# One core's decoder layer: order of the first loads, TensorE in program order, and the last norm's column product

## The chip, the cores and the metric

The kernel runs on one core of a Trainium2 chip. Five engines work from queues of their own: TensorE (PE: matmuls, with weight loads on PEld), VectorE (DVE), ScalarE (ACT), GpSimd (POOL) and SyncE (SP, which issues the loads and stores). The metric is the device time of one execution in microseconds; lower is better. Matmul operands come from on-chip memory (SBUF), sums are kept in eight banks of PSUM.

## The reference

One layer on x of 512 tokens by 1024, in float32:

```
x = x + 0.5 * SwiGLU_1(RMSNorm(x))
h = RMSNorm(x);  P = h @ W_in
A = NSA attention (compressed, selected and sliding-window branch, 16 heads)
B = W_conv_out(Bg * conv3(Cg * xin))
x = x + W_out(sigmoid(ga) * (A @ W_nsa_out) + sigmoid(gb) * B)
x = x + 0.5 * SwiGLU_2(RMSNorm(x))
out = RMSNorm(x)      # x * rsqrt(mean(x^2) + eps) * gain
```

A SwiGLU is silu(x @ w_gate) * (x @ w_up), then @ w_down, with 2816 features (22 blocks f0 to f21 of 128).

## The kernel before, in words

x is held transposed: eight tiles d0 to d7 of 128 features by 512 tokens. Each float32 operand is split into a high part, rounded on ACT (`whi`, `hi`, `gh`), and the rest, taken on DVE (`wlo`, `lo`, `gl`); a product is the sum hi*hi + hi*lo + lo*hi, three matmuls to one chunk of 128.

The first feed-forward takes f0 to f3 as plain products. For g0, u0 and g1 the function `first` loads weights and x piece by piece, in the order of a list `items`, splits each as it comes and issues a matmul as soon as its row of weights and x are there. From f4 on, and for all of the second feed-forward, gate and up of one block f are computed together by a scheme of Strassen's kind, called here a quartet: seven half-size block products, in the written order a11, s1, s2, s3, a12, s4, a22, of 12 matmuls of 256 columns each, on four PSUM banks p1, p5, p6, p7. DVE makes the weights' sums (`ws`) and their low parts, joins the products (u, y, e) and multiplies by the norm's scale. Two things set waits: s4 adds to bank p5, from which u (line 553) reads the product s1, so s4 must come behind u; and a quartet's weights sit in pools of two or three buffers.

A norm is: squares on ACT, added up by DVE into `ssum`; a column product on PE (`col`) that sums over the partitions; v on DVE; the power -1/2 on POOL; a split of the result into rh and rl on DVE; and PE matmuls that spread it over the partitions (`rbp`). The scale is put on a product's output, so a product need not wait for its norm.

The last product (`down`, d7) is done in two halves of 256 tokens, each followed by its part of the norm (`final`) and eight outputs, two to a store of 256 KB.

What sets the order: every engine takes its instructions in the order in which they were queued. In the first parts of the two feed-forwards (`begin1`, `begin2`) that is the order of the code, by `manual_schedule`; elsewhere a scheduler orders each engine's instructions by its own costs, and may put blocks of the next quartets ahead of a block that it thinks late. In `begin2`, whose quartet f0 holds the middle norm, hooks 3, 4 and 5 put the norm's steps between the blocks. SP's loads keep the list's order.

Of the kernel before, what the change touches and what calls it, by code (L numbers as in the profile page):

```python
# [13 lines left out]
ENGINES = {mybir.EngineType.PE, mybir.EngineType.DVE, mybir.EngineType.Activation}  # L14
# [28 lines left out]
def f32(ap):  # L43
    return ap.bitcast(F32)


class Kernel:
# [17 lines left out]
    def fixed(self):  # L65

        const = self.const
        self.small = const.tile([P, SM_N], F32, name="small")
        self.one = const.tile([P, 1], F32, name="one")
        self.ident = const.tile([P, P], F32, name="ident")  # L70
        self.mhalf = const.tile([P, 4], F32, name="mhalf")
        self.identr = const.tile([P, P], F32R, name="identr")
        const.tile([P, PAD], F32, name="pad")
# [18 lines left out]
    def gemm(self, ps, chunks, xs, stepwise=False):  # L92
# [17 lines left out]
    def chain(self, ps, ops):  # L110
        for n, (w, x) in enumerate(ops):
            self.nc.tensor.matmul(ps, w, x, start=n == 0, stop=n == len(ops) - 1)  # L112
# [20 lines left out]
    def constants(self):  # L133
        nc = self.nc
        nc.scalar.dma_start(out=self.small, in_=self.io["small"])
        nc.vector.memset(self.one, 1.0)
# [8 lines left out]
        nc.gpsimd.tensor_copy(self.identr, self.ident)  # L145
# [9 lines left out]
    def square(self, x, d, c=slice(0, S)):  # L155
        nc = self.nc
        if d == 0:
            self.ssum = self.slot(name="ssum")
            nc.scalar.activation(self.ssum, x, AF.Square)
        else:  # L160
            sq = self.slot(name="sq")
            nc.scalar.activation(sq[:, c], x[:, c], AF.Square)
            nc.vector.tensor_add(self.ssum[:, c], self.ssum[:, c], sq[:, c])

    def rnorm(self, blocks=range(4)):

        steps = self.rnorm_steps(blocks)
        r = next(steps)
        next(steps)
        return r, next(steps)  # L170

    def rnorm_steps(self, blocks=range(4)):
        nc = self.nc
        b0, b1 = blocks[0], blocks[-1] + 1
# [6 lines left out]
        yield r  # L181
        hi, lo = (self.tmp.tile([P, 4], F32R, name=n, bufs=2) for n in ("rh", "rl"))
        nc.vector.tensor_copy(hi[:, b0:b1], r[:, b0:b1])
        nc.vector.tensor_sub(lo[:, b0:b1], r[:, b0:b1], f32(hi[:, b0:b1]))
        yield

        def spread():
            rb = self.ps.tile([P, S], F32, tag="ps", name="rbp")
            for b in blocks:
                self.chain(rb[:, b * P:(b + 1) * P],  # L190
                           [(t[:, b:b + 1].to_broadcast([P, P]), self.identr) for t in (hi, lo)])
            return rb

        yield spread
# [12 lines left out]
    def ffn1(self):  # L207

        nc, wgu = self.nc, self.io["wgu1"]
        rb = self.slot(name="rb")  # L210
        with self.tc.tile_pool(name="st", bufs=2) as self.st:
            with self.tc.manual_schedule(engines=ENGINES):
                hid, now = self.begin1(wgu, rb)
            self.tiles(wgu, now, hid, PLAIN, rb)
        self.xg, self.xf = [], {}
        self.down(self.io["wd1"], hid, rb, 1)

    def begin1(self, wgu, rb):
# [3 lines left out]
        out["g0"], out["u0"], out["g1"] = self.first([wgu[0, :, 0], wgu[0, :, 1], wgu[1, :, 0]])  # L222
# [24 lines left out]
        spread = self.rnorm()[1]  # L247
        product("u1", self.pmm, "mm")
        rbp = spread()
# [32 lines left out]
    def ffn2(self):  # L282
# [5 lines left out]
        with self.tc.tile_pool(name="st", bufs=2) as self.st:  # L288
            merged, now = self.merge(wgu, parts)
            self.xg = []  # L290
            rb = self.slot(name="rb")
            with self.tc.manual_schedule(engines=ENGINES):
                now = self.begin2(wgu, merged, now, rb, hid)
            self.tiles(wgu, now, hid, 1, rb)
# [23 lines left out]
    def begin2(self, wgu, merged, now, rb, hid):  # L318
# [29 lines left out]
        norm = self.rnorm_steps()  # L348

        def end():  # L350
            nc.scalar.copy(rb, next(norm)())

        hid.append(self.quartet(now[0], later[1], True, rb, {3: lambda: next(norm), 4: lambda: next(norm), 5: end}))
# [11 lines left out]
    def down(self, wd, hid, rb, nxt):  # L365
        nc = self.nc
        hs = []
        for d in range(KD):
# [6 lines left out]
            last = d == KD - 1 and nxt is None  # L375
            for c in ((slice(0, 256), slice(256, S)) if last else (slice(0, S),)):
                ps = self.pmm.tile([P, S], F32, tag="mm", name="dn")
                self.gemm(ps[:, c], chunks, [(h[:, c], l[:, c]) for h, l in hs], d == 0)
                x, t = self.x[d], self.slot(name="dt")
                nc.vector.tensor_mul(t[:, c], ps[:, c], rb[:, c])  # L380
                nc.vector.scalar_tensor_tensor(x[:, c], t[:, c], 0.5, x[:, c], op0=ALU.mult, op1=ALU.add)
                if last:
                    self.square(x, d, c)
                    self.final(c)
            if not last:
                self.residual(d, nxt)
# [143 lines left out]
    def quartet(self, w, steps, odd, rb, hooks):  # L530
# [23 lines left out]
        more()  # L554
        self.block(p7, w["s3"], "t3", True)
        hook(3)
# [3 lines left out]
        hook(4)  # L560
# [4 lines left out]
        hook(5)  # L565
        if hooks:
            nc.vector.tensor_mul(g[:, c0], half(p1), rb[:, c0])
        add(e[:, c1], u[:, c0], half(p5))
        nc.vector.tensor_mul(g[:, c1], e[:, c1], rb[:, c1])
        nc.scalar.activation(g, g, AF.Silu)  # L570
        self.block(p7, w["a22"], "t4", False)
        add(y[:, c0], u[:, c0], half(p7))
# [3 lines left out]
    def first(self, srcs):  # L576
# [10 lines left out]
        def load_w(t, k, n):  # L587
            raws[t, k, n] = raw = self.slot(name="w0")[:, :n * P]
            nc.sync.dma_start(out=raw, in_=srcs[t][:, k * P:(k + n) * P])
# [7 lines left out]
        for kind, *args in items:  # L597
# [4 lines left out]
            else:  # L602
                t, k, n = args
                hi, lo = self.split(raws[t, k, n], n=n * P)
                for j in range(n):
                    ws[t, k + j] = hi[:, j * P:(j + 1) * P], lo[:, j * P:(j + 1) * P]
# [133 lines left out]
    def keys_compressed(self, hid):  # L740
# [13 lines left out]
        self.chain(ps[:, :64], ops)  # L754
# [37 lines left out]
    def quad(self, n):  # L792
# [12 lines left out]
        self.chain(st, [(k[:, g, 96 - 32 * h:224 - 32 * h], self.qs[4 * n + h]) for h in range(4) for k in self.kc])  # L805
# [145 lines left out]
    def mixing(self):  # L951
# [3 lines left out]
        self.r, spread = self.rnorm()  # L955
        kc = self.proj(0)
        self.rb = self.slot(name="rb")
        nc.scalar.copy(self.rb, spread())
# [90 lines left out]
    def final(self, c):  # L1049
        nc = self.nc  # L1050
        rb = self.rnorm(range(c.start // P, c.stop // P))[1]()
        for d in range(0, KD, 2):
            o = self.slot(name="o").rearrange("p (d t) -> p d t", d=2)
            for j in range(2):
                nc.vector.scalar_tensor_tensor(o[:, j], self.x[d + j][:, c], self.gain(3, d + j), rb[:, c],
                                               op0=ALU.mult, op1=ALU.mult)
            nc.sync.dma_start(out=self.io["out"][d:d + 2, :, c].rearrange("d p t -> p d t"), in_=o)
# [57 lines left out]
```

## Time and profile before

| | |
|---|---|
| median of 3 runs | 1299.24 us (1299.22 to 1299.62) |
| the profiled execution | 1299.69 us |
| its span, first to last instruction | 1297.9 us |
| mean granted clock of TensorE | 0.996 |
| PE busy | 1282.4 us, 99% |
| DVE, ACT, POOL busy | 965.8, 613.1, 9.3 us |
| the chain that ended last | PE 97%, DVE 1%, DMA 1% |

Busy time is the time in which an engine had work; the granted clock is TensorE's, as a share of 2.4 GHz. A timeline row has the start, the duration and, in brackets, the idle time before it and the instruction that ended it. Matmul durations overlap: the distance of two starts is the pace, not the duration.

### The profile page before, as it was taken

What the parts mean: (1) busy time and instruction counts of PE and PEld (TensorE: products, weight loads), DVE (VectorE), ACT (ScalarE), POOL (GpSimd) and SP (SyncE); (2) the same over time, 40 slices, a digit from 0 to 9 for tenths busy, and PEclk for the clock granted to TensorE, in tenths of its full rate; (3) what the DMA queues carried; (4) which work ended last, traced back from release to release, by engine and by line L of the source; (5) the groups of instructions that cost most, each with busy time, mean ns of one, the idle gap of its engine ahead of it and who ended that gap; (6) DMA issues with size and microseconds to landing.
All of it is one profiled execution on the core that took longest, in us unless ns stands there. A gap on an engine that the chain in (4) does not pass through costs nothing.

```text
span 1297.9 us, 19392 instructions
## 1 busy us (share of the span) xinstructions
PE 1282.4 (99%) x7660; PEld 1139.7 (88%) x7660; DVE 965.8 (74%) x1790; ACT 613.1 (47%) x1039; POOL 9.3 (1%) x33
## 2 busy tenths in 40 slices
PE   9999999999999999999999999999999999999996
PEld 7899999888888988888888888888899999998886
DVE  7899999834376377787787767766799999986334
ACT  7644444622245455555555547634544444454220
POOL 1000000000000000000000000000000000000000
PEclk9999999999999999999999999999999999999999
DMA  5233333343425422122121111243223333333321
GB/s 197 90 122 98 102 111 109 99 122 106 126 83 173 136 68 81 50 65 65 55 76 49 66 66 49 65 130 121 91 92 104 99 113 100 112 94 102 95 84 65
DMA packets 38987, 124.39 MB, mean 96 GB/s; under 512 B 4336, under 2 KB 6768, under 8 KB 38896
## 3 DMA queue, kind: packets, MB, share of 16 engines
q1 hardware_dynamic: 38752, 123.09, 29.8%
q8 instruction: 60, 0.98, 0.3%
q14 instruction: 31, 0.25, 0.1%
q10 hardware_dynamic: 144, 0.06, 0.0%
HBM read 118.94 MB, written 4.19 MB: 95 GB/s over the span
## 4 chain that ended last, share of the span: by engine, by line
PE 97%; DVE 1%; DMA 1%; ACT 0%; POOL 0%; SPq 0%; issue 0%; POOLq 0%; DVEq 0%
PE st L528 30%; PE pj L112 22%; PE dn L112 19%; PE yb L112 3%; PE wo L112 3%; PE ya L112 3%; PE s L857 3%; PE pt L882 3%; PE gu L112 2%; PE pv L900 2%; PE pv L899 2%; PE gu L612 1%; PE sct L112 1%; DMA w<-wgu 0%; PE nat L667 0%; PE nat L668 0%
## 5 line engine op out<-in xcount | busy, mean ns | idle before, releaser
L86 ACT CAST whi<-wraw 128x1024 fp32r<-128x1024 f32 (+2 forms) x140 | 143.0, 1022 | 243.5 <-PE dn L112 105.9
L87 DVE TENSOR_TENSOR wlo<-wraw,whi 128x1024 fp32r<-128x1024 f32 (+2 forms) x140 | 165.9, 1185 | 103.9 <-PE dn L112 67.9
L528 PE MATMUL st<-xf,whi 128*128 128x256 f32 x1248 | 228.4, 283 | 0.5 <-DVE u L553 0.5
L528 PEld LDWEIGHTS st<-xf,whi 128*128 128x128 f32 x1248 | 194.7, 192 | 0.7 <-DVE u L553 0.7
L528 PE MATMUL st<-xf,wlo 128*128 128x256 f32 x624 | 176.7, 283 | 0.0
L112 PE MATMUL pj<-hi,whi 128*128 128x512 f32 x416 | 165.1, 397 | 0.0
L112 PE MATMUL pj<-lo,whi 128*128 128x512 f32 x416 | 163.0, 392 | 0.0
L112 PE MATMUL dn<-hi,whi 128*128 128x512 f32 (+1 forms) x374 | 139.6, 378 | 0.0
L112 PE MATMUL dn<-lo,whi 128*128 128x512 f32 (+1 forms) x374 | 138.8, 377 | 0.0
L528 PE MATMUL st<-xf,gh 128*128 128x256 f32 x640 | 119.8, 284 | 1.0 <-ACT gh L431 1.0
L528 PEld LDWEIGHTS st<-xf,wlo 128*128 128x128 f32 x624 | 119.7, 192 | 0.5 <-DVE wlo L435 0.4
L431 ACT CAST whi<-ws 128x1024 fp32r<-128x1024 f32 x78 | 81.1, 1048 | 64.1 <-DVE ws L447 60.6
L112 PE MATMUL pj<-hi,wlo 128*128 128x512 f32 x416 | 102.9, 389 | 0.0
L528 PEld LDWEIGHTS st<-xf,gh 128*128 128x128 f32 x640 | 100.4, 192 | 1.6 <-ACT gh L431 1.4
L435 DVE TENSOR_TENSOR wlo<-ws,whi 128x1024 fp32r<-128x1024 f32 x78 | 95.0, 1217 | 0.3 <-ACT whi L431 0.2
L112 PE MATMUL dn<-hi,wlo 128*128 128x512 f32 (+1 forms) x374 | 94.9, 377 | 0.0
L112 PEld LDWEIGHTS pj<-hi,wlo 128*128 128x128 f32 x416 | 78.0, 188 | 16.2
L528 PE MATMUL st<-xf,gl 128*128 128x256 f32 x320 | 90.6, 284 | 0.8 <-DVE gl L435 0.8
L112 PEld LDWEIGHTS pj<-lo,whi 128*128 128x128 f32 x416 | 78.2, 188 | 14.5
L112 PEld LDWEIGHTS pj<-hi,whi 128*128 128x128 f32 x416 | 78.2, 188 | 14.5 <-ACT hi L129 0.4
L863 ACT ACTIVATE p<-p,st 128x512 f32<-128x512 f32 (+3 forms) x128 | 70.3, 552 | 28.0 <-DVE st L860 28.0
L112 PEld LDWEIGHTS dn<-lo,whi 128*128 128x128 f32 x374 | 70.4, 188 | 13.8 <-DVE lo L127 0.7
(249 smaller groups left out, 2451.8 us busy)
## 6 DMA issues: line engine op xcount, KB each, us to landing
wraw<-wgu SPq DMA_DIRECT2D x83, 512.0 KB, 3.6
wraw<-win SPq DMA_DIRECT2D x52, 512.0 KB, 3.5
wraw<-wd SPq DMA_DIRECT2D x32, 512.0 KB, 3.5
wraw<-wd SPq DMA_DIRECT2D x16, 384.0 KB, 3.2
wraw<-cw SPq DMA_DIRECT2D x8, 512.0 KB, 3.8
wraw<-wconv SPq DMA_DIRECT2D x8, 512.0 KB, 3.4
wraw<-wnsa SPq DMA_DIRECT2D x8, 512.0 KB, 3.6
wraw<-wout SPq DMA_DIRECT2D x8, 512.0 KB, 3.7
```

Source lines behind the costliest of these rows:

```text
L86: nc.scalar.copy(hi[:, :n], raw[:, :n])
L87: nc.vector.tensor_sub(lo[:, :n], raw[:, :n], f32(hi[:, :n]))
L112: self.nc.tensor.matmul(ps, w, x, start=n == 0, stop=n == len(ops) - 1)
L431: copy(hi[:, c], src)
L435: sub(lo[:, c], src, f32(hi[:, c]))
L528: mm(o, lhs, rhs, start=start and k + n == 0, stop=k == 3 and n == 2, skip_group_check=not start)
L612: nc.tensor.matmul(ps, w, x, start=k + n == 0, stop=k == KD - 1 and n == 2)
L857: nc.tensor.matmul(out, q, k[:, bs[0]:bs[-1] + 1, :n], start=part == 0, stop=part == 1)
L863: nc.scalar.activation(o, o, AF.Exp, bias=st[:, 0, b, i:i + 1], scale=-1.0, accum_out=st[:, 1, b, i:i + 1])
L882: nc.tensor.transpose(ps[:, c:c + P], where[b, i][:, j * P:(j + 1) * P], self.ident)
L899: nc.tensor.matmul(o[:, j * P:], v, hi, start=False, stop=False)
L900: nc.tensor.matmul(o[:, j * P:], v, lo, start=False, stop=n == 7)
```

## The change

It does four things. (1) `first` loads g0 and u0 together, one DMA for both, and in smaller rows of the product: chunk 0 of both, x0, chunk 0 of g1, x1, chunk 1 of both, and so on; 16 weight and x loads, where there were 15, of the same bytes. (2) In a norm the column product's ones are 1/1024 (so v only adds eps), the result r is spread as plain float32, without rh and rl. (3) PE keeps program order through all quartets of both feed-forwards and through the last product; ACT and DVE keep it, as before, in the two first parts only. In `begin2` the norm's hooks move: column product behind s3, spreading behind a22. (4) For the last norm, x times the gain is made on ACT ahead of the sum; the column product of each half is done in two parts, first over `ssum` of d0 to d6, ahead of the half's matmuls, then over the square of d7; the first half's second part and spreading stand at matmuls 24 and 44 of the second half's 66. An output pair is one DVE multiplication of 128x512.

The diff, cut to its core:

```diff
-ENGINES = {mybir.EngineType.PE, mybir.EngineType.DVE, mybir.EngineType.Activation}
+MATMULS = {mybir.EngineType.PE}
+OTHERS = {mybir.EngineType.DVE, mybir.EngineType.Activation}
...
-        self.chain(ps, ops)
+        self.chain(ps, ops, between or {})
+    def chain(self, ps, ops, between):
         for n, (w, x) in enumerate(ops):
+            between.get(n, lambda: None)()
             self.nc.tensor.matmul(ps, w, x, start=n == 0, stop=n == len(ops) - 1)
...
+    def column(self, blocks, stop):
         col = self.ps.tile([P, S], F32, tag="ps", name="col")
         for b in blocks:
-            nc.tensor.matmul(col[:, b:b + 1], self.ssum[:, b * P:(b + 1) * P], self.one, start=True, stop=True)
+            self.nc.tensor.matmul(col[:, b:b + 1], self.ssum[:, b * P:(b + 1) * P], self.one,
+                                  start=b == blocks[0], stop=stop and b == blocks[-1], skip_group_check=True)
+        return col
+    def power(self, col, blocks, sq=None):
+        nc = self.nc
+        if sq is not None:
+            for b in blocks:
+                nc.tensor.matmul(col[:, b:b + 1], sq[:, b * P:(b + 1) * P], self.one,
+                                 start=False, stop=b == blocks[-1], skip_group_check=True)
...
-        nc.vector.tensor_scalar(v[:, b0:b1], col[:, b0:b1], 1.0 / D, EPS, op0=ALU.mult, op1=ALU.add)
+        nc.vector.tensor_scalar_add(v[:, b0:b1], col[:, b0:b1], EPS)
         nc.gpsimd.tensor_tensor(out=r[:, b0:b1], in0=v[:, b0:b1], in1=self.mhalf[:, b0:b1], op=ALU.pow)
-        nc.vector.tensor_copy(hi[:, b0:b1], r[:, b0:b1])
-        nc.vector.tensor_sub(lo[:, b0:b1], r[:, b0:b1], f32(hi[:, b0:b1]))
...
-            with self.tc.manual_schedule(engines=ENGINES):
-                now = self.begin2(wgu, merged, now, rb, hid)
-            self.tiles(wgu, now, hid, 1, rb)
+            with self.tc.manual_schedule(engines=MATMULS):
+                with self.tc.manual_schedule(engines=OTHERS):
+                    now = self.begin2(wgu, merged, now, rb, hid)
+                self.tiles(wgu, now, hid, 1, rb)
...
-        hid.append(self.quartet(now[0], later[1], True, rb, {3: lambda: next(norm), 4: lambda: next(norm), 5: end}))
+        hid.append(self.quartet(now[0], later[1], True, rb, {0: reduce, 2: spread}))
...
+    def last(self, chunks, hs, rb):
+        halves = slice(0, 256), slice(256, S)
+        out = [[self.gained(d, c) for d in range(0, KD, 2)] for c in halves]
+        before = {}
+        for n, c in enumerate(halves):
+            blocks = range(2 * n, 2 * n + 2)
+            col = self.column(blocks, False)
+            ps = self.pmm.tile([P, S], F32, tag="mm", name="dn")
+            self.gemm(ps[:, c], chunks, [(h[:, c], l[:, c]) for h, l in hs], between=before)
+            self.half_step(KD - 1, ps, rb, c)
+            steps = self.final(c, col, blocks, out[n])
+            before = {24: lambda: next(steps), 44: lambda: next(steps)}
+        next(steps)
+        next(steps)
...
-        items = [("w", 0, 0, 1), ("x", 0), ("w", 0, 1, 3), ("x", 1), ("w", 1, 0, 4), ("x", 2), ("w", 2, 0, 4), ("x", 3),
-                 ("w", 0, 4, 4), ("x", 4), ("w", 1, 4, 4), ("x", 5), ("w", 2, 4, 4), ("x", 6), ("x", 7)]
+        both, third = (0, 1), (2,)
+        items = [("w", both, 0, 1), ("x", 0), ("w", third, 0, 1), ("x", 1), ("w", both, 1, 1), ("w", third, 1, 3), ("x", 2),
+                 ("w", both, 2, 2), ("x", 3), ("w", both, 4, 2), ("x", 4), ("w", third, 4, 4), ("x", 5), ("w", both, 6, 2),
+                 ("x", 6), ("x", 7)]
...
+    def final(self, c, col, blocks, out):
+        nc = self.nc
+        x = self.x[KD - 1][:, c]
+        sq = self.slot(name="sq")
+        nc.scalar.activation(sq[:, c], x, AF.Square)
+        nc.scalar.activation(out[-1][:, 1], x, AF.Copy, scale=self.gain(3, KD - 1))
+        r = self.power(col, blocks, sq)
+        yield
+        rb = self.spread(r, blocks)[:, None, c].to_broadcast([P, 2, 256])
+        for d, o in enumerate(out):
+            nc.vector.tensor_mul(o, o, rb)
+            nc.sync.dma_start(out=self.io["out"][2 * d:2 * d + 2, :, c].rearrange("d p t -> p d t"), in_=o)
+        yield
```

What that moves on PE, at three places. The first is in the first feed-forward, from the end of a12 of f4 (bank `st_664` before, `st_662` after) to the start of s4 (`st_665` before, `st_663` after). Before:

```order
L528 MATMUL st_664<-xf_552,gl_575 128x256
L528 MATMUL st_792<-xf_477,gh_660 128x256
L528 MATMUL st_792<-xf_477,gl_661 128x256
L528 MATMUL st_792<-xf_536,gh_660 128x256 x2
L528 MATMUL st_792<-xf_536,gl_661 128x256
L528 MATMUL st_793<-xf_330,whi_703 128x256 x2
L528 MATMUL st_794<-xf_337,whi_703 128x256 x2
L528 MATMUL st_920<-xf_327,gh_788 128x256 x2
L528 MATMUL st_793<-xf_330,wlo_704 128x256
L528 MATMUL st_793<-xf_414,whi_703 128x256 x2
L528 MATMUL st_793<-xf_414,wlo_704 128x256
L528 MATMUL st_665<-xf_346,whi_620 128x256 x2
```

and of the change:

```order
L553 MATMUL st_662<-xf_550,gh_572 128x256 x2
L553 MATMUL st_662<-xf_550,gl_573 128x256
L553 MATMUL st_663<-xf_352,whi_618 128x256 x2
L553 MATMUL st_663<-xf_352,wlo_619 128x256
L553 MATMUL st_663<-xf_428,whi_618 128x256 x2
L553 MATMUL st_663<-xf_428,wlo_619 128x256
L553 MATMUL st_663<-xf_494,whi_618 128x256 x2
```

The rows on `st_792`, `st_793`, `st_794` and `st_920` are blocks of f5 and f6; they stood between the two and are gone from there: s4 follows a12 at once.

The second is in `begin2`, from the end of a12 of the quartet f0 to s4 (`st_9188` before, `st_9181` after; `st_9467` is a bank of f2, whose a11 is on `gh_9335`). Before:

```order
L528 MATMUL st_9187<-xf_9175,gl_8467 128x256
L528 MATMUL st_9467<-xf_8814,gh_9335 128x256 x2
L528 MATMUL st_9467<-xf_8814,gl_9336 128x256
L528 MATMUL st_9467<-xf_8918,gh_9335 128x256 x2
L528 MATMUL st_9467<-xf_8918,gl_9336 128x256
L528 MATMUL st_9188<-xf_8871,sh_8676 128x256 x2
L528 MATMUL st_9188<-xf_8871,sl_8677 128x256
```

and of the change:

```order
L553 MATMUL st_9180<-xf_9071,gl_8458 128x256
L553 MATMUL st_9180<-xf_9168,gh_8457 128x256 x2
L553 MATMUL st_9180<-xf_9168,gl_8458 128x256
L553 MATMUL st_9181<-xf_8864,sh_8667 128x256 x2
L553 MATMUL st_9181<-xf_8864,sl_8668 128x256
L553 MATMUL st_9181<-xf_8969,sh_8667 128x256 x2
```

The first half of f2's a11 is gone from between them (f1 comes next in the change), and so are the other rows of f1 and f2 that stood between s4 and a22.

The third is the start of the last product's first half (256 columns), behind d6's matmuls of 512 columns. Before:

```order
L112 MATMUL dn<-lo,whi 128x512
L112 MATMUL dn<-hi,wlo 128x512 x6
L112 MATMUL dn<-hi,whi 128x256
L112 MATMUL dn<-lo,whi 128x256
L112 MATMUL dn<-hi,whi 128x256
```

and of the change:

```order
L114 MATMUL dn<-lo,whi 128x512
L114 MATMUL dn<-hi,wlo 128x512 x6
L175 MATMUL col<-one,ssum 128x1 x2
L114 MATMUL dn<-hi,whi 128x256
L114 MATMUL dn<-lo,whi 128x256
```

The column product over `ssum`, which before stood far down in the second half, is now ahead of the first half's matmuls.

## Rows read from the trace of the kernel before

**Rows 1.** The page's first part: engine, busy us (share of the span), instructions

```profile
PE 1282.4 (99%) x7660; PEld 1139.7 (88%) x7660; DVE 965.8 (74%) x1790; ACT 613.1 (47%) x1039; POOL 9.3 (1%) x33
```

**Rows 2.** PE's waits: line, engine waited for; us in total, times, longest

```profile
PE col L177 <- DVE ssum L163: 1.9, 1, 1.9
PE st L528 <- DVE u L553: 0.5, 1, 0.5
```

**Rows 3.** The chain of waits: start us, us, what

```profile
9.97 15.05 PE gu L612 x65
32.26 21.85 PE gu L112 x96
59.61 176.81 PE st L528 x1467
```

**Rows 4.** Timeline of PE at the first loads: start us, us, instruction [idle before]

```profile
5.44 0.47 PE L612 MATMUL gu<-hi 128*128 128x512 f32 x1
7.21 0.50 PE L612 MATMUL gu<-hi 128*128 128x512 f32 x1 [0.83 <-ACT hi L129]
9.25 0.50 PE L612 MATMUL gu<-hi 128*128 128x512 f32 x1 [0.75 <-ACT hi L126]
```

**Rows 5.** Timeline of DVE, first blocks of the first feed-forward

```profile
28.56 0.17 DVE L183 CAST rh<-r 128x4 fp32r<-128x4 f32 x1 [1.14 <-POOL r L180]
58.34 1.22 DVE L435 TENSOR_TENSOR wlo<-ws,whi 128x1024 fp32r<-128x1024 f32 x1
63.94 0.41 DVE L553 TENSOR_TENSOR u<-u,st 128x256 f32<-128x256 f32 x1
```

**Rows 6.** Busy time by stretch: us, PE, PEld, DVE, ACT, POOL, PEclk, DMA share, GB/s

```profile
60.00:70.00 10.00, 10.00 (x81) 9.61 (x81) 10.00 (x18) 5.53 (x8) 0.00 (x0) 1.00 0.33 107
```

**Rows 7.** Timeline of PE behind the middle norm's column product

```profile
943.77 0.28 PE L528 MATMUL st<-xf,gl 128*128 128x256 f32 x1
945.06 0.50 PE L528 MATMUL st<-xf,gh 128*128 128x256 f32 x2 [1.02 <-ACT gh L431]
946.32 0.39 PE L528 MATMUL st<-xf,gl 128*128 128x256 f32 x1 [0.76 <-DVE gl L435]
947.03 0.63 PE L528 MATMUL st<-xf,sh 128*128 128x256 f32 x2
```

**Rows 8.** Timeline of DVE in the same stretch

```profile
945.04 1.22 DVE L435 TENSOR_TENSOR gl<-wraw,gh 128x1024 fp32r<-128x1024 f32 x1 [0.18 <-ACT gh L431]
946.19 0.41 DVE L553 TENSOR_TENSOR u<-u,st 128x256 f32<-128x256 f32 x1
```

**Rows 9.** Busy time by stretch, after those waits

```profile
946.00:951.00 5.00, 4.68 (x26) 4.68 (x27) 4.74 (x11) 1.43 (x2) 1.01 (x1) 0.66 0.46 147
```

**Rows 10.** Timeline of PE, the last product's two halves

```profile
1268.99 0.28 PE L112 MATMUL dn<-hi,whi 128*128 128x256 f32 x1
1276.90 0.28 PE L112 MATMUL dn<-hi,whi 128*128 128x256 f32 x1
1278.95 0.60 PE L177 MATMUL col<-one,ssum 128*128 128x1 f32 x4
1280.86 0.33 PE L112 MATMUL rbp<-identr,rh 128*128 128x128 f32 x1 [0.59 <-DVE rh L183]
```

**Rows 11.** Timeline of DVE, from the last-but-one block to the end

```profile
1269.80 0.95 DVE L87 TENSOR_TENSOR wlo<-wraw,whi 128x768 fp32r<-128x768 f32 x1
1272.05 0.69 DVE L163 TENSOR_TENSOR ssum<-ssum,sq 128x512 f32<-128x512 f32 x1 [0.70 <-ACT sq L162]
1287.07 0.42 DVE L380 TENSOR_TENSOR dt<-dn,rb 128x256 f32<-128x256 f32 x1 [2.21 <-PE dn L112]
1288.43 0.42 DVE L163 TENSOR_TENSOR ssum<-ssum,sq 128x256 f32<-128x256 f32 x1 [0.48 <-ACT sq L162]
1291.60 3.22 DVE L1055 SCALAR_TENSOR_TENSOR o<-x,small,rbp 128x256 f32<-128x256 f32 x8 [0.64 <-PE rbp L112]
```

**Rows 12.** The page's DMA issues: KB each, median us to landing

```profile
out<-o SPq DMA_DIRECT2D x8, 256.0 KB, 2.2
```

More of the change, by code (lines that the diff above doesn't have):

```diff
@@ L153, in gain, with square @@
         return self.small[:, c:c + 1]
[L155 removed]
+    def square(self, x, d):
         nc = self.nc
@@ L161, in square @@
             sq = self.slot(name="sq")
[L162 to L174, printed above, removed]
+            nc.scalar.activation(sq, x, AF.Square)
@@ L194, in rnorm_steps, with spread @@
-        yield spread
+        return r
+    def spread(self, r, blocks=range(4)):
+        rb = self.ps.tile([P, S], F32, tag="ps", name="rbp")
+        for b in blocks:
+            self.nc.tensor.matmul(rb[:, b * P:(b + 1) * P], r[:, b:b + 1].to_broadcast([P, P]), self.ident,
+                                  start=True, stop=True)
+        return rb
     def plain(self, gate, up, rb, hid):
@@ L246, in begin1 @@
         weights("g2")
-        spread = self.rnorm()[1]
+        r = self.rnorm()
         product("u1", self.pmm, "mm")
-        rbp = spread()
+        rbp = self.spread(r)
         forms(1)
@@ L347, in begin2, with reduce, spread @@
             self.square(x, d)
-        norm = self.rnorm_steps()
-        def end():
-            nc.scalar.copy(rb, next(norm)())
-        hid.append(self.quartet(now[0], later[1], True, rb, {3: lambda: next(norm), 4: lambda: next(norm), 5: end}))
+        norm = {}
+        def reduce():
+            norm["r"] = self.rnorm()
+        def spread():
+            nc.scalar.copy(rb, self.spread(norm["r"]))
+        hid.append(self.quartet(now[0], later[1], True, rb, {0: reduce, 2: spread}))
         return later
@@ L374, in down, with half_step @@
                     hs += [self.split(t) for t in hid[k:k + n]]
[L375 to L386, printed above, removed]
+            if d == KD - 1 and nxt is None:
+                with self.tc.manual_schedule(engines=MATMULS):
+                    self.last(chunks, hs, rb)
+                break
+            ps = self.pmm.tile([P, S], F32, tag="mm", name="dn")
+            self.gemm(ps, chunks, hs, d == 0)
+            self.half_step(d, ps, rb, slice(0, S))
+            self.residual(d, nxt)
+    def half_step(self, d, ps, rb, c):
+        nc = self.nc
+        x, t = self.x[d], self.slot(name="dt")
+        nc.vector.tensor_mul(t[:, c], ps[:, c], rb[:, c])
+        nc.vector.scalar_tensor_tensor(x[:, c], t[:, c], 0.5, x[:, c], op0=ALU.mult, op1=ALU.add)
+    def last(self, chunks, hs, rb):
[5 more added lines that the diff above has]
+            col = self.column(blocks, False)
+            ps = self.pmm.tile([P, S], F32, tag="mm", name="dn")
+            self.gemm(ps[:, c], chunks, [(h[:, c], l[:, c]) for h, l in hs], between=before)
[4 more added lines that the diff above has]
+        next(steps)
     def load(self, wgu, f, apart=False):
@@ L553, in quartet @@
         add(u[:, c1], u[:, c0], half(p5))
-        more()
+        if not hooks:
+            more()
         self.block(p7, w["s3"], "t3", True)
-        hook(3)
+        hook(0)
         add(y[:, c1], u[:, c1], half(p7))
@@ L564, in quartet, with first @@
         self.block(p5, w["s4"], "b22", False)
-        hook(5)
+        add(e[:, c1], u[:, c0], half(p5))
+        if not hooks:
+            nc.vector.tensor_mul(g[:, c1], e[:, c1], rb[:, c1])
+            nc.scalar.activation(g, g, AF.Silu)
+        self.block(p7, w["a22"], "t4", False)
+        hook(2)
+        add(y[:, c0], u[:, c0], half(p7))
         if hooks:
             nc.vector.tensor_mul(g[:, c0], half(p1), rb[:, c0])
[L568 to L572, printed above, removed]
+            nc.vector.tensor_mul(g[:, c1], e[:, c1], rb[:, c1])
+            nc.scalar.activation(g, g, AF.Silu)
+            more()
         nc.vector.tensor_mul(g, g, y)
         return g
-    def first(self, srcs):
+    def first(self, wgu):
         nc = self.nc
@@ L602, in first @@
             else:
[L603 to L606, printed above, removed]
+                ts, k, n = args
+                hi, lo = self.split(raws[ts, k].rearrange("p t m -> p (t m)"), n=len(ts) * n * P)
+                for j in range(len(ts) * n):
+                    ws[ts[j // n], k + j % n] = hi[:, j * P:(j + 1) * P], lo[:, j * P:(j + 1) * P]
             for t, ps in enumerate(pss):
@@ L1047, in run, with gained @@
         self.ffn2()
-    def final(self, c):
-        nc = self.nc
[L1051 to L1057, printed above, removed]
+    def gained(self, d, c):
+        o = self.slot(name="o").rearrange("p (d t) -> p d t", d=2)
+        for j in range(2):
+            if d + j < KD - 1:
+                self.nc.scalar.activation(o[:, j], self.x[d + j][:, c], AF.Copy, scale=self.gain(3, d + j))
+        return o
+    def final(self, c, col, blocks, out):
+        nc = self.nc
+        x = self.x[KD - 1][:, c]
[9 more added lines that the diff above has]
+        yield
 @with_exitstack
```

43 lines of the change are left out of this document (18 added, 25 removed).

## Prediction

> **What bounds the kernel now.** I read the page's busy times first: TensorE (PE) is busy 1282.4 of the 1297.9 us span [rows 1], so only about 15.5 us, before the first product, in a few gaps, and behind the last product, are not matmul. Nothing in the change takes matmuls out of the products; the question is what becomes of those gaps. The chain of waits says the same: one unbroken piece of PE work follows another, for instance 1467 matmuls of the quartets in 176.81 us [rows 3], which also gives the pace: 176.81/1467 = 0.1205 us for 256 columns (a block of 12 is 1.45 us, a quartet of 84 is 10.1), and 21.85/96 = 0.228 us for 512. VectorE (DVE) is at 74% over the span, but the stretch 60 to 70 us shows it busy 10.00 of 10.00 while PE is also full [rows 6]: there both are at their limit, and PE hides nothing for DVE. The waits of PE themselves, with their releasers, come last [rows 2, 4, 7, 10].
>
> The profiled execution took 1299.69 us, 1.79 more than its span and 0.45 above the median of the runs, 1299.24. I work out differences in the profiled execution and add them to the median. About 0.2% (2.6 us) is what a measurement can tell from no change.
>
> **First loads.** The first product starts at 5.44, and the 72 matmuls end at 9.97+15.05 = 25.02 [rows 3, 4]. At 0.228 they need 16.4 us, so 25.02-5.44-16.4 = 3.2 us are lost, 0.83 and 0.75 of it where PE stands still for a split (rows marked hi) [rows 4]. The new order brings k0 of both g0 and u0 with x0, so with about 1 MB on the chip 18 matmuls are allowed where before 12 were (before: three chunks of g0 with x0 and x1, two of u0; now two of each of the three). I estimate that 1.0 of 3.2 us stays, a gain of 2.2. Bounds: 3.2 if no gap is left; a loss of 1 if the pieces, now twice as many rows of 512 B and 1 KB, come later by as much as one of the old gaps.
>
> The Trainium skill, "DMA: Bandwidth & Descriptors", section "Specifications", wants at least 512 B per transfer for line rate; the new pieces of one k-chunk stand just on that edge. No row of before has a load with 512 B runs on its path, so nothing here shows it; by the rule the gain of the loads stands.
>
> **First feed-forward in program order.** This is where the gain goes. The scheduler of before fills PE with blocks of f5 and f6 while DVE is late with f4. In program order PE must do s4 of f4 as its sixth block, and s4 writes on the bank from which u (L553) reads: u runs at 63.94 to 64.35 [rows 5]. DVE is full there [rows 6] and does the same work in the same order up to that u, so u moves only as far as DVE's earlier part does. That part loses the cast and the difference of rnorm: the idle 1.14 for POOL goes (the next fm doesn't need r), and the two small operations of 0.17 [rows 5], together 1.4. From the first loads DVE gains little, as the eight x come in their old order; I take 0.5 (bounds 0 and 3.2). So u ends at 64.35-1.9 = 62.45. PE, meanwhile, starts f4 at 32.26+21.85 = 54.11 before [rows 3], now at 51.9. Five blocks of 1.45 would be done at 59.1; the low half of s3's weights (58.34+1.22-1.9 = 57.66 [rows 5]) takes 1.4 of the wait, u the other 1.9. Behind it wait a22 and all of f5, on which DVE, itself late, doesn't yet depend. s4 starts at 62.45; before, PE had done the work of five blocks at 54.11+7.23 = 61.34, without a stop. The place as a whole, first loads included, costs **+1.1** (bounds: +1.6 if DVE gains nothing from the loads, -2.2 if it gains all of their 3.2 or the wait vanishes). After it the quartets take 10.1 us of PE and about 9.5 of DVE, so no further stop is expected.
>
> The Trainium skill, "TensorE: Matmul & The Clock Gate", section "Step-by-step: what each phase is for", states that matmuls stay in program order and only weight loads are pulled ahead. The trace agrees: at 945.06 the hoisted block waits 1.02 us for gh, and the ready s4 of the earlier quartet stays behind it [rows 7]. By that rule nothing but the written order can fill the wait for u.
>
> Price of the clock: behind the waits of 1.02 and 0.76 [rows 7] PE's granted clock means 0.66 over the five us from 946 [rows 9], at 1.2 instead of 2.4 GHz for most of them: 5.00 x 0.34 = **1.7 us** lost. Two waits of 1.4 and 1.9 near 60 us may do the same; I put that at a bit under even and leave it out of the likeliest sum.
>
> **Middle norm.** Before, PE ends a12 at about 943.9, is stopped 1.02 and 0.76, and starts s4 at 947.03, having done six hoisted matmuls (0.7 us) in between: 2.4 lost [rows 7]; then 1.7 by the clock [rows 9], and 0.49 at a later u [rows 2]. Now no f2 block stands in the way, but DVE's order is unchanged here: gl of f2 (945.04, 1.22) is still ahead of u (946.19 to 946.60) [rows 8], and s4 waits for u: idle 943.9 to 946.65, 2.75. The later 0.49 goes. With the clock falling as before that is 2.4+0.5-2.75 = a gain of 0.2; the reduction comes 1 us earlier on DVE, worth up to 0.6 more. I take **-0.5**; if the clock stays up, -2.0.
>
> **Last half step.** For each half the column product of x0 to x6 now stands ahead of the half's matmuls. For the first half it needs ssum of d6, which DVE ends at 1272.05+0.69 = 1272.74 [rows 11], because dt, a 0.95 us weight split, x and ScalarE's square all lie between d6's last matmul and it. Before, PE went straight on at 1268.99 [rows 10]. Behind the waiting product stand all 132 matmuls of both halves, and everything up to the last store waits for them. PE is idle 1268.99 to 1272.74, 3.75 us, plus the product's own 0.47 (its 0.60 less overlap): the first half starts 4.2 late, at 1273.2, and lasts 1276.90-1268.99 = 7.9 [rows 10], to 1281.1. The second half takes 66 x 0.1205 = 7.95, two column products (0.47 each) and the spread (about 0.6 as before): it ends at 1290.6, against 1287.07 [rows 11], +3.5 (before, 0.59 of waiting for rh lay inside [rows 10], which goes).
> From there the chain shrinks: ssum (0.45) and the two hi/lo steps (0.2) leave the 4.53 us from dt at 1287.07 to the first o at 1291.60 [rows 11]; PE's wait of 1.9 for ssum [rows 2] becomes one for the square. First o at 1294.5. A stored pair costs DVE 0.60 (a two-input 128x512 like ssum's 0.69, pipelined) instead of 3.22/4 = 0.80. The stores (four of 256 KB per half, 2.2 us to land [rows 12]) ended 1297.9-1292.4 = 5.5 after the first pair; if they set the pace, the end is 1294.5+0.6+5.5 = 1300.6, +2.7; if DVE does, last o at 1296.9 plus the old 1297.9-1294.8 = 3.1: +2.1. I take **+2.6**. The 14 scalings lie on ScalarE behind d6's square, beside PE's 16 us of matmuls, and cost nothing; without that cover they would cost 14 x about 0.4. The clock: 3.75 us idle is twice the stop that brought it down before, so I add the 1.7 less a little for the first column product, **+1.5** (bounds 0 and 1.7).
>
> The rest: x0's POOL copy of the identity is off the path; ffn2's later quartets keep their 10.1 us of PE. Zero, and no gain, as PE has no wait there [rows 2].
>
> **Sum.** 1.1 - 0.5 + 2.6 + 1.5 = +4.7: 1299.24+4.7, say **1304.0**. Own range 1302 to 1306.
>
> **Rivals.**
> - *The clock falls in the first feed-forward too* (two waits of 1.4 and 1.9 there against 1.02 and 0.76 that sufficed): +1.7, 1305.7. Against it: PE works 1.45 us between the two.
> - *DVE follows the first loads* (not slower). Place: u of f4. DVE has waits of its own before 40 us, for splits and PE's column product; if PE's earlier end moves all of DVE by the loads' gain, u comes 3 us earlier. It decides from the point where u ends before 60.0: then s4 waits less than 1 us, the place gives -2 to -2.2, and the sum is -2.1-0.5+2.6 = 0, plus 1.5 where the tail's clock falls: 1299.2 to 1300.7; with the clock up in the middle too, 1297. Against it: DVE at 10.00 of 10.00 [rows 6] with a 1.14 us gap as the only large one that goes.
> - *No fall of the clock anywhere.* 1.1-2.0+2.6 = +1.7: 1301.0. For it: the fall at 946.7 came after two stops and a stretch of sparse matmuls, not one stop. Against: the idle stretch at 1269 is longer than both together.
> - *The loads don't bring their rows sooner* (smaller pieces land late): the loads' gain is 0, PE reaches s4's place at 61.3 and waits for u (62.95), +1.6 instead of 1.1, and the stops may fall together: 1304.5 to 1306.
>
> The rule of the skill's page on the clock ("What's actually happening" in "TensorE: Matmul & The Clock Gate": the slow state is the default and work releases it) is borne out by [rows 9], with 0.66 after the stops; it speaks for the second term of the tail.
>
> **Chances.** Forecast 0.40; clock falls in both 0.24; loads late 0.08; no fall 0.12; DVE follows 0.16. Slower by over 0.2% (above 1301.8): the first three and a few of the fourth, 0.73. Faster by over 0.2% (below 1296.6): half of the last, with the clock up, 0.09. Within: 0.18. The range 1299.0 to 1307.0 leaves out most of the faster cases and the sum of all falls with a late load.
>
> **What would show it.** Right: PE idle at about 1269 to 1272.7 ahead of the column product, first half from 1273; a stop at s4 of f4 for u near 60 to 62.5; a single stop of 2.7 us at 944 instead of three; rows at half clock behind the tail's stop. Wrong: the column product running without a wait, u of f4 before 60, or new PE waits for weights in the later quartets, which I put at zero.

## The result: 1306.11 us, slower by 0.5%

Four runs of the changed kernel gave 1305.19 to 1308.14 us, median 1306.11, against 1299.42 for the kernel before: a ratio of 1.0054 (1.0036 to 1.0071), +6.7 us where +4.7 was forecast. The profiled execution took 1308.14 us, 2.0 above that median (span 1306.4, clock 0.992); it is 8.45 longer than the profiled execution of before.

The page's busy times, against [rows 1]: PE is busy 4.5 us longer in a span that is 8.5 longer, with 8 instructions more.

```profile
PE 1286.9 (99%) x7668; PEld 1144.8 (88%) x7668; DVE 963.9 (74%) x1771; ACT 619.8 (47%) x1056; POOL 9.1 (1%) x32
```

PE's waits, against [rows 2] (line, engine waited for; us in total, times, longest):

```profile
PE st L553 <- DVE u L578: 4.5, 2, 2.6
PE col L175 <- DVE ssum L164: 3.6, 1, 3.6
PE st L553 <- DVE wlo L460: 1.5, 2, 0.8
PE col L183 <- ACT sq L1093: 1.4, 1, 1.4
```

u is now waited for twice, 1.90 and 2.61 us, and one column product waits 3.6 for ssum. Where the time is lost is read by comparing the same instruction in both traces.

**First feed-forward.** The chain of waits has the long piece of quartets (start, length):

```profile
63.02 176.00 PE st L553 x1452
```

It ends at 239.02, before at 59.61+176.81 = 236.42 [rows 3]: 2.60 later. PE's timeline shows the three stops at s1, s3 and s4 of f4:

```profile
54.39 0.38 PE L553 MATMUL st<-xf,wlo 128*128 128x256 f32 x1 [0.77 <-DVE wlo L460]
58.22 0.39 PE L553 MATMUL st<-xf,wlo 128*128 128x256 f32 x1 [0.69 <-DVE wlo L460]
63.02 0.80 PE L553 MATMUL st<-xf,whi 128*128 128x256 f32 x2 [1.90 <-DVE u L578]
```

and DVE's the low half and u that end the last two, against [rows 5]:

```profile
56.94 1.22 DVE L460 TENSOR_TENSOR wlo<-ws,whi 128x1024 fp32r<-128x1024 f32 x1
62.55 0.42 DVE L578 TENSOR_TENSOR u<-u,st 128x256 f32<-128x256 f32 x1
```

u starts 1.39 earlier than at 63.94, not 1.9; s4 starts at 63.02, forecast 62.45.

**Middle norm.** PE's timeline has one stop where [rows 7] had two, and DVE's the reason: f2's low half is still ahead of u, as in [rows 8].

```profile
944.33 0.95 PE L175 MATMUL col<-one,ssum 128*128 128x1 f32 x8
949.43 0.50 PE L553 MATMUL st<-xf,sh 128*128 128x256 f32 x2 [2.61 <-DVE u L578]
```

```profile
947.82 1.23 DVE L460 TENSOR_TENSOR gl<-wraw,gh 128x1024 fp32r<-128x1024 f32 x1 [0.18 <-ACT gh L456]
948.96 0.42 DVE L578 TENSOR_TENSOR u<-u,st 128x256 f32<-128x256 f32 x1
```

**Last half step.** PE's timeline (against [rows 10]) and DVE's (against [rows 11]):

```profile
1275.46 1.01 PE L175 MATMUL col<-one,ssum 128*128 128x1 f32 x4 [3.64 <-DVE ssum L164]
1286.64 0.50 PE L175 MATMUL col<-one,ssum 128*128 128x1 f32 x4
1297.45 0.61 PE L183 MATMUL col<-one,sq 128*128 128x1 f32 x4 [1.42 <-ACT sq L1093]
1299.16 1.22 PE L195 MATMUL rbp<-ident,r 128*128 128x128 f32 x4 [1.10 <-POOL r L188]
```

```profile
1272.47 0.95 DVE L87 TENSOR_TENSOR wlo<-wraw,whi 128x768 fp32r<-128x768 f32 x1
1274.72 0.69 DVE L164 TENSOR_TENSOR ssum<-ssum,sq 128x512 f32<-128x512 f32 x1 [0.70 <-ACT sq L163]
1296.07 0.42 DVE L394 TENSOR_TENSOR dt<-dn,rb 128x256 f32<-128x256 f32 x1
1300.41 2.48 DVE L1099 TENSOR_TENSOR o<-o,rbp 128x512 f32<-128x512 f32 x4 [2.09 <-PE rbp L195]
```

The first column product waits 3.64 us for ssum. The weight split that stood at 1269.80 now stands at 1272.47, 2.67 late, so between the first feed-forward's end and there only 0.07 was lost; from it to the end of the span 1306.4-1272.47 = 33.9 pass, before 1297.9-1269.80 = 28.1: the tail costs 5.8. (The tail is the stretch from that split to the end.)

**The clock.** Busy time by stretch (columns as in [rows 6]; the third number from the end is the granted clock), behind each of the three stops:

```profile
60.00:70.00 10.00, 8.10 (x55) 7.90 (x54) 8.79 (x15) 4.40 (x6) 0.00 (x0) 0.83 0.32 107
949.00:954.00 5.00, 4.57 (x25) 4.58 (x26) 3.56 (x8) 1.20 (x2) 1.01 (x1) 0.66 0.48 146
1275.00:1282.00 7.00, 6.54 (x32) 6.54 (x33) 0.41 (x1) 5.28 (x14) 0.00 (x0) 0.53 0.00 0
```

TensorE ran at 1.2 instead of 2.4 GHz in parts of each. At 1275 to 1282 that is up to 7.00 x (1-0.53) = 3.3 us, twice the price that [rows 9] had given.

### The profile page after: what moved, and what is told of

It is laid out like the page before. It is cut to its first block, busy times and chain, and to the rows that moved or that the text cites. A ratio compares the mean times of both kernels' runs of the same rounds, so it can differ in the third digit from the quotient of the medians.

```text
span 1306.4 us, 19418 instructions
## 1 busy us (share of the span) xinstructions
PE 1286.9 (99%) x7668; PEld 1144.8 (88%) x7668; DVE 963.9 (74%) x1771; ACT 619.8 (47%) x1056; POOL 9.1 (1%) x32
## 4 chain that ended last, share of the span: by engine, by line
PE 94%; DVE 2%; ACT 2%; issue 1%; DMA 1%; SPq 0%; POOLq 0%; POOL 0%; DVEq 0%; ACTq 0%
PE st L553 31%; PE pj L114 22%; PE dn L114 18%; PE yb L114 3%; PE wo L114 3%; PE ya L114 3%; PE s L889 3%; PE pt L914 3%; PE pv L932 2%; PE pv L931 2%; PE sct L114 1%; DMA w<-wgu 0%; ACT xf L524 0%; DVE wlo L87 0%; PE nat L699 0%
```

## The experiments

Medians and ratios are to the kernel before, run on the same chip.

| kernel | median us | ratio, 95% |
|---|---|---|
| the change | 1306.11 | 1.0054 (1.0036 to 1.0071) |
| e1 sum late | 1299.66 | 1.0004 (0.9995 to 1.0014) |
| e2 first feed-forward hoisted | 1303.08 | 1.0030 (1.0018 to 1.0041) |
| e3 both | 1296.75 | 0.9981 (0.9971 to 0.9990) |
| e4 stop filled | 1302.47 | 1.0027 (1.0017 to 1.0037) |
| e5 loads alone | 1299.45 | 0.9997 (0.9988 to 1.0006) |
| e6 e3 with ffn2 hoisted | 1296.13 | 0.9970 (0.9959 to 0.9982) |
| e7 e3 with u first | 1293.90 | 0.9950 (0.9937 to 0.9962) |
| e8 order in ffn1 alone | 1303.22 | 1.0024 (1.0015 to 1.0033) |
| e9 norm alone | 1298.53 | 0.9993 (0.9984 to 1.0001) |
| e10 loads and norm | 1296.70 | 0.9977 (0.9968 to 0.9986) |

**e1, the column product later.**

```diff
-            col = self.column(blocks, False)
+            late = {}
+            before[40 - 28 * n] = lambda: late.update(col=self.column(blocks, False))
...
+            col = late["col"]
```

> The change with one edit: the column product over ssum is issued 40 matmuls into the first half's product (12 into the second's) instead of ahead of it. My theory: the tail's loss is PE's stop ahead of that product (3.64 us) and the half clock behind it (0.50 for some 6 us). Without the stop the tail ends about 0.5 us earlier than in the kernel before (hi/lo steps, ssum and shorter outputs gone, a wait of 0.59 gone, one more column product), so the whole is 1299.4 + 2.6 (first feed-forward) - 0.1 - 0.5 = 1301.4. Rival, that the new chain of the norm itself (square as column product, outputs of 512 columns) is the longer one and the stop is hidden: 1305 to 1306.

1299.66: the stop ahead of the product was the tail's loss, and the rival is out. The gain is 1.7 more than expected, for two reasons. The first is the tail; DVE's timeline of it:

```profile
1271.00 0.95 DVE L87 TENSOR_TENSOR wlo<-wraw,whi 128x768 fp32r<-128x768 f32 x1
1287.98 0.42 DVE L394 TENSOR_TENSOR dt<-dn,rb 128x256 f32<-128x256 f32 x1
1291.82 2.48 DVE L1101 TENSOR_TENSOR o<-o,rbp 128x512 f32<-128x512 f32 x4 [1.58 <-PE rbp L195]
```

From the split at 1271.00 to the end (1297.8) it is 26.8 us, before 28.1: without the stop the new tail is worth 1.3, not 0.5. The shorter norm alone gives 0.4 to 0.5 of it (e9 and e10, with the old outputs, take 27.7 and 27.6); the rest belongs to the new outputs and the divided column product, which no run parts. From dt to the first o it takes 3.84 (before 1291.60-1287.07 = 4.53); in the change it took 4.34, since the spread there ran at a lower clock (1.22 us for it at 1299.16, against 0.71 in e1).

The second reason is the clock. Behind the middle norm's stop, which is as long as in the change, it stayed at 1.00 in this execution, though behind the stop for u of f4 it fell as in the change:

```profile
60.00:70.00 10.00, 8.10 (x56) 7.90 (x55) 8.89 (x16) 4.32 (x6) 0.00 (x0) 0.83 0.33 105
949.00:954.00 5.00, 4.54 (x38) 4.54 (x39) 4.55 (x10) 1.71 (x3) 1.01 (x1) 1.00 0.48 152
```

From the end of the first feed-forward's quartets (239.11) to the split it took 1031.89 us, against 1033.45 in the change.

**e2, blocks hoisted in the first feed-forward.**

```diff
-        with self.tc.tile_pool(name="st", bufs=2) as self.st, self.tc.manual_schedule(engines=MATMULS):
-            with self.tc.manual_schedule(engines=OTHERS):
+        with self.tc.tile_pool(name="st", bufs=2) as self.st:
+            with self.tc.manual_schedule(engines=MATMULS | OTHERS):
```

> The change with one edit: in the first feed-forward PE's program order ends with begin1, so the scheduler may put blocks of f5 and f6 ahead of s4 of f4 as it did before. My theory: the 2.6 us that the change has lost by the end of the quartets are the waits at s1, s3 and s4 of f4 and the half clock behind them; with blocks hoisted PE has no wait there and keeps most of the first loads' 2.2: the first feed-forward ends about 1.5 to 2.2 earlier than before, 1306.1 - 2.6 - 1.9 = 1301.6. Rival, DVE is the bound of the stretch and PE loses the loads' gain in any order: about 0 against before there, 1303.5.

1303.08, 3.0 less than the change and 0.4 less than the rival's time; the estimate of 4.5 was too high. The trace decides between the two: the wait for u of f4 is gone, and the chain's piece of quartets ends at 62.27+172.66 = 234.93.

```profile
62.27 172.66 PE st L553 x1436
```

That is 1.5 earlier than before, as my theory had it, where the rival had about 0; and it is 4.1 before the change's profiled execution, which had the fall of the clock as well. The estimate took the loss of 2.6 from that execution and subtracted it from the median, which lies 2.0 lower: the two don't fit together.

**e3, both edits.**

> Both edits of the two kernels before it (column product late, scheduler in the first feed-forward). My theory: the two losses add and nothing else is left but the middle norm (-0.1): 1299.4 - 1.9 - 0.1 - 0.5 = 1296.9. Rival by which DVE bounds the first feed-forward: 1298.8. Rival by which the new norm chain is long: 1301 or more.

1296.75, as expected, but partly by luck: in the profiled execution, 1.3 below that median, the first feed-forward gave 1.45, the stretch behind it 1.41 (the clock stayed at 1.00 there) and the tail 1.3, where 1.9, 0.1 and 0.5 had been added up. The chain of waits:

```profile
5.61 17.35 PE gu L646 x72
62.63 172.34 PE st L555 x1434
```

The first product now ends at 5.61+17.35 = 22.96, 2.06 before the old 25.02: the loads do at the start what was forecast (2.2). The quartets end at 234.97, 1.45 earlier than before. "DMA: Bandwidth & Descriptors" of the Trainium skill (section "Specifications") puts line rate at 512 B and up; the trace agrees so far that no loss is seen, though more of the first loads have rows of 512 B than before.

**e4, the tail's stop filled.**

```diff
+        idle = self.pv.tile([P, S], F32, tag="pv", name="idle")
+        for _ in range(30):
+            self.nc.tensor.matmul(idle[:, :256], chunks[0][0][:, 0, :], hs[0][0][:, :256], start=True, stop=True)
```

> The change with 30 matmuls of 256 columns added on an otherwise idle PSUM bank ahead of the tail's first column product, whose result nothing uses: 30 x 0.12 = 3.6 us of work in the place of the 3.64 us stop. My theory, that the stop itself brings TensorE's clock down: the clock stays at 1.00 behind it and the time falls by the clock's loss alone, 1.7 to 3.3 us, to 1303 to 1304.4. Rival, the clock falls for another reason, or the half rate costs nothing as something else waits: 1306.

1302.47, 3.6 less than the change, though the half's matmuls still start only when ssum is there. The stretch that had 0.53 is at full clock:

```profile
60.00:70.00 10.00, 8.09 (x68) 7.88 (x67) 9.97 (x18) 4.50 (x7) 0.00 (x0) 1.00 0.33 107
1269.00:1282.00 13.00, 12.94 (x104) 12.58 (x103) 2.85 (x4) 6.83 (x16) 0.00 (x0) 1.00 0.01 2
```

DVE's split, from which the tail is counted, stands at:

```profile
1270.69 0.95 DVE L87 TENSOR_TENSOR wlo<-wraw,whi 128x768 fp32r<-128x768 f32 x1
```

To the end (1301.9) that is 31.2, +3.1 against before, and 2.7 less than the change's 33.9. So the tail is 3.1 for the stop and the order, and 2.7 for the clock. The runs that weren't profiled agree: over the whole span the granted clock was 0.992 to 0.994 in the change's four executions and 0.995 to 0.998 in the nine of e4. The same trace tells of the first feed-forward: the stop for u is there, as long as in the change, yet the clock stays at 1.00 (60 to 70 above). PE's timeline, and the chain's piece:

```profile
62.79 0.51 PE L556 MATMUL st<-xf,whi 128*128 128x256 f32 x2 [1.91 <-DVE u L581]
```

```profile
62.79 174.52 PE st L556 x1452
```

The quartets end at 237.31, 1.7 before the change's 239.02 with the fall, and 0.9 after the old 236.42. Of the 1.7, 1.5 are the clock (the same 1452 matmuls took 174.52 and 176.00 us) and 0.2 the earlier start of s4. The place thus costs 0.9 or 2.6, mainly by whether the clock falls in that execution. The Trainium skill says of TensorE's slow start ("TensorE: Matmul & The Clock Gate", "What's actually happening") that it varies between runs of one kernel. These two traces show something like it for a stop of 1.9 us inside a kernel.

**e5, the first loads alone.** The function `first` of the change in the kernel before.

> The kernel before with the new first loads alone (old norm, old orders). In the run with both edits the quartets of the first feed-forward ended 1.45 us earlier than before. My theory: the loads give their 2.2 at the start, and the scheduler's hoisted blocks carry most of it through, while DVE, which here keeps its cast, difference and the wait for POOL (1.4 us), now is closer behind PE: 1299.2 - 1.5 = 1297.7, at worst 1298.7 with some waits for low halves. Rival, the gain of that run came from the shorter norm on DVE and not from the loads: 1299.2.

1299.45, no gain: my theory failed, the rival held so far. DVE still waits for POOL at the norm's cast (28.56 in [rows 5]), u is where it was (63.94), and the quartets end at 63.56+172.83 = 236.39, as before. PE is early and stands still instead: 1.12 us idle between 30 and 60, where before it had none.

```profile
28.62 0.17 DVE L183 CAST rh<-r 128x4 fp32r<-128x4 f32 x1 [1.14 <-POOL r L180]
63.92 0.42 DVE L553 TENSOR_TENSOR u<-u,st 128x256 f32<-128x256 f32 x1
```

```profile
63.56 172.83 PE st L528 x1436
```

```profile
30.00:60.00 30.00, 28.88 (x149) 24.17 (x149) 26.54 (x51) 18.75 (x35) 0.00 (x0) 1.00 0.28 91
```

**e6, the second feed-forward hoisted too.** e3 with begin2 alone in program order, as before the change.

> The kernel with both edits, and PE's program order taken away from the second feed-forward too (it ends with begin2), so the first half of f2's a11 stands ahead of s4 of f0 again. My theory: the middle norm is one stop of 2.6 in program order against three smaller ones without, and the clock may fall in both; 1296.75 within 0.6. Rival, program order hides a loss in the later quartets: 1295 or less; or it saves more than the stop costs: 1298 or more.

1296.13: 0.62 below e3, at the edge of the expected 0.6, with intervals that overlap; the rivals' times are out. Program order in the later quartets neither gains nor loses anything that these runs can tell.

**e7, u first.**

```diff
         self.block(p5, w["s1"], "t1", True)
-        more()
+        if not hooks:
+            more()
...
         add(u[:, c1], u[:, c0], half(p5))
-        if not hooks:
-            more()
+        more()
...
-        nc.vector.tensor_scalar_add(v[:, b0:b1], col[:, b0:b1], EPS)
+        self.last_v = nc.vector.tensor_scalar_add(v[:, b0:b1], col[:, b0:b1], EPS)
...
             def low():
-                for c, src in zip(cols, srcs):
-                    sub(lo[:, c], src, f32(hi[:, c]))
+                with self.tc.issue_after(self.last_v.ins):
+                    for c, src in zip(cols, srcs):
+                        sub(lo[:, c], src, f32(hi[:, c]))
```

> The kernel with both edits, and in the quartet f0 of the second feed-forward the weight step behind s1 (low half of f1's a11 and a12, differences) is issued behind u, and f2's low half behind v. DVE's work ahead of u falls by 1.2 + 2 x 0.6 + 1.2 = 3.6 us, so u ends before a12 does. My theory: PE's stop of 2.61 at s4 goes, and with it the fall of the clock that some executions show there (up to 1.7): 1296.75 - 2.6 - 0 to 0.9 = 1293.2 to 1294.2. Rival, the stop moves to the spreading of r or to f1's weights: 1295.5 or more.

1293.90, as expected, and 5.5 less than before (ratio 0.9950, 0.9937 to 0.9962). PE's timeline has 0.29 left of the stop, at a22, and the spread follows without a wait. In the traces, both at full clock there, the stretch from the quartets' end to the tail's split is 2.4 shorter than in e3. This version is faster than both kernels.

```profile
945.31 0.50 PE L556 MATMUL st<-xf,a22h 128*128 128x256 f32 x2 [0.29 <-DVE y L586]
946.84 1.05 PE L195 MATMUL rbp<-ident,r 128*128 128x128 f32 x8
```

**e8, program order in the first feed-forward alone.** The kernel before, with tiles f4 to f21 under the change's program order on PE.

> The kernel before with program order on PE in the first feed-forward alone (old loads, old norm, old tail). My theory: PE reaches s4 of f4 at 61.3 and u ends at 64.35 as in the trace of before, so it waits 3.0 in all at s1, s3 and s4: 1299.2 + 3.0 = 1302.2, and up to 1.7 more where the clock falls: 1302.2 to 1303.9. It is the measure of what the order itself costs, which in the change is partly paid by the loads and the shorter norm. Rival, the change's loss there comes from the loads' earlier PE meeting DVE, and order alone costs under 1: 1300.

1303.22: as expected, and the rival is out. The quartets end at 64.54+174.52 = 239.06 in the profiled execution, +2.6, and the clock stays at full behind the stop for u. PE's timeline, the busy time of the stretch and the chain's piece:

```profile
64.54 0.50 PE L529 MATMUL st<-xf,whi 128*128 128x256 f32 x2 [1.90 <-DVE u L554]
```

```profile
60.00:70.00 10.00, 8.10 (x67) 7.89 (x67) 10.00 (x18) 5.00 (x7) 0.00 (x0) 1.00 0.34 116
```

```profile
64.54 174.52 PE st L529 x1452
```

**e9, the shorter norm alone.** The kernel before, without rh and rl.

> The kernel before with the norm's shorter form alone (r spread as plain float32, no cast, no difference); old loads, old orders, old tail. The loads alone left u of f4 where it was (63.92 against 63.94) and gained nothing. My theory now: PE's start sets one bound of the first feed-forward and DVE's frame another, and each part of the change moves only one. Here DVE is 1.4 us earlier at u, PE has no wait to give back (none between 10 and 236 us): nothing there, and 0.2 to 0.4 from the two steps missing in the tail: 1299.0 to 1299.2. Rival, the shorter norm alone gives the 1.5: 1297.7.

1298.53, 0.5 below the expected times; the interval includes no change. In this execution the first product ended 0.5 later than before (PE waited 1.70 for the split of an x, and the granted clock was 0.89 over the first ten us), and u came 0.54 later than before; taking off the late product, it would stand where it did. ACT's timeline shows why the norm alone moves nothing here: the copy of the spread scale waits 2.39 for PE, which hasn't come so far, and DVE then waits 3.36 for ACT.

```profile
32.80 0.59 ACT L248 COPY rb<-rbp 128x512 f32<-128x512 f32 x1 [2.39 <-PE rbp L187]
```

```profile
34.37 1.22 DVE L87 TENSOR_TENSOR wlo<-wraw,whi 128x1024 fp32r<-128x1024 f32 x1 [3.36 <-ACT whi L86]
64.48 0.42 DVE L550 TENSOR_TENSOR u<-u,st 128x256 f32<-128x256 f32 x1
```

**e10, loads and norm.** e9's and e5's edits together.

> The kernel before with the new first loads and the shorter norm, all orders and the tail as before. My theory of two bounds: PE starts 2.2 earlier and DVE's frame moves by 1.4, so the first feed-forward ends 1.4 earlier as in the runs with hoisted blocks, and the tail gives 0.2 to 0.4: 1299.2 - 1.7 = 1297.5. Rival, the 1.5 came from the new quartet's order of DVE's steps: 1299.0.

1296.70, 2.7 less than before, where the loads gave 0.0 and the norm 0.9. The same split waits 0.87 for ACT instead of 3.36, u is 1.76 earlier than in [rows 5], and the quartets end at 62.32+172.34 = 234.66, 1.76 earlier than before:

```profile
32.12 1.23 DVE L87 TENSOR_TENSOR wlo<-wraw,whi 128x1024 fp32r<-128x1024 f32 x1 [0.87 <-ACT whi L86]
62.18 0.42 DVE L550 TENSOR_TENSOR u<-u,st 128x256 f32<-128x256 f32 x1
```

```profile
62.32 172.34 PE st L525 x1434
```

## Why the prediction was right, and where its sizes were off

The direction, and the place and cause of the three large stops, were right; the sum was 2 us short. The measured 1306.11 lies just above the narrower range that the sum named (1302 to 1306) and inside the wider one (1299.0 to 1307.0). The four terms as measured in the change's trace (2.6, 0.1, and 5.8 for the tail and its clock) make up the 8.5 by which that execution is longer. With e4's 0.9 for the first of them, where the clock stayed up, they make 6.8, about the median's 6.7; what the clock did in the executions without a trace isn't known stop by stop.

- *First loads*: forecast 2.2 at the start, measured 2.06 (e3). That DVE would gain 0.5 from them by themselves was wrong (e5). Its frame is held by two things: PE's spread of the scale (u1's product stands ahead of it) and DVE's own wait for POOL. The loads move the first, the shorter norm the second; alone neither brought u of f4 forward (e5; e9), together they brought it 1.4 to 1.8 (e3, e10), and 1.39 in the change, where 1.9 was forecast. How much of that is whose can't be said.
- *Program order in the first feed-forward*: the step "s4 must wait for u" held, with s4 at 63.02 instead of 62.45. Forecast +1.1; measured +0.9 without a fall of the clock (e4), +2.6 with it. The rival with the fall, which I gave 0.24, was what the profiled execution did. By e8 the order costs 2.6 by itself at full clock, and the change's loads and norm pay 1.7 of it. The wait for low halves, forecast as 1.4 at s3, came as 0.77 at s1 and 0.69 at s3. e2 takes the loss away.
- *Middle norm*: forecast -0.5, or -2.0 if the clock stays up; measured up to the tail's split within 0.1 of nothing where it falls, as it had before, and -1.5 where it stays up (e1). The single stop of 2.61 was forecast as 2.75. It wasn't needed: e7.
- *Tail*: the stop was forecast at 3.75 and measured 3.64, the tail without the clock at +2.6 and measured +3.1 (e4). The mis-sized term is the clock: forecast +1.5, measured +2.7. I had taken the price of [rows 9], 1.7, for a fall after shorter stops; behind the longer one the half rate lasted nearly twice as long. The gain of the new tail without the stop was undersized the other way: e1 shows 1.3 where its expectation had 0.5, but in the change the stop buried it.

The price of 1.7 itself was TensorE's time at the lower clock, not what reached the end. From the end of the first feed-forward's quartets to the tail's split the kernel before, with the fall of [rows 9], took 1033.38 us; e5, with the same code in that stretch and the clock at 1.00 behind its stops, took 1269.05-236.39 = 1032.66. Its busy time by stretch, and DVE's timeline:

```profile
945.00:950.00 5.00, 4.12 (x30) 3.69 (x30) 4.65 (x10) 2.49 (x4) 1.01 (x1) 1.00 0.37 111
```

```profile
1269.05 0.95 DVE L87 TENSOR_TENSOR wlo<-wraw,whi 128x768 fp32r<-128x768 f32 x1
```

So there the fall cost 0.7; behind the change's single stop it cost 1.6 (1033.45 against e1's 1031.89).

That matmuls hold everything behind them in program order (the Trainium skill, "TensorE: Matmul & The Clock Gate", section "Step-by-step: what each phase is for", as the prediction cited it) is borne out by e1, in which 40 of the half's matmuls ran without a wait once they stood ahead of the column product, and by e2, in which only another order of issue took the wait for u away. The row that the prediction gave for it doesn't show it: s4 wasn't ready at 945.06, as u, behind which it must come, ended at 946.60 [rows 8].

Three smaller slips in the prediction's working: the 12 matmuls that 1 MB allowed before are two chunks each of g0 and u0, not three and two. The kernel before, too, has a load with rows of 512 B on its path, its first one (chunk 0 of g0). And the rival in which DVE follows comes to 1297.7 with the clock up, not 1297, and neither is below 1296.6, so the 0.09 for "faster" had no sum behind it.

Open: why the clock fell in two executions behind the stop of 1.90 us for u of f4 (the change, e1) and not in two others (e4, e8). The change and e4 have the same instructions there, but not the same stops ahead of it: the two with the fall had waited 0.77 and 0.80 us at s1, e8 0.58 and e4 less than 0.1. Four traces don't settle whether that is the reason.

## What to carry to other kernels

Where an engine that runs in program order is the bound, ask of each instruction put ahead of its work which producer ends last, and how long that producer's chain is behind the bound engine's own last result: here dt, a weight split, x, a square and a sum, 3.6 us, and half clock on top. A gain in the start of a stretch is kept only if every engine that feeds the stretch starts earlier too; two edits that measure 0.0 and 0.9 us alone (the 0.9 not clear of nothing) were worth 2.7 together. Filler work in the tail's stop was worth 3.6 us by the medians, 2.7 of it in the tail by the traces; moving the waiting product behind 40 matmuls was worth 6.5.

## What was not expected of the hardware

A stop of the same length, 1.90 us (1.91), in front of the same matmuls was followed by a granted clock of 0.83 over ten us in one execution and 1.00 in another. For those matmuls that is a difference of 1.5 us. The executions of one kernel lie far apart: the change's four over 3.0 us (1305.19 to 1308.14), e7's five, with the stop at the middle norm gone, over 1.0 (1293.08 to 1294.07). That the clock makes the spread isn't shown for the executions without a trace.
